# Measured durations in the list that orders the convolution block

## The chip, the cores and the metric

The kernel runs on one NeuronCore of a Trainium2 chip. The metric is the device time of one execution in microseconds (us); lower is better. The core has five engines that run side by side and meet through semaphores: TensorE (PE in the profile, its weight loads PEld), VectorE (DVE), ScalarE (ACT), GpSimd (POOL) and SyncE (SP). POOL and SP mostly issue DMAs here.

## The reference, cut to what matters

One step of a two-layer trunk over a prompt of 512 tokens and 8 x 4 decode tokens, model width 1024, all in float32. Layer 0 mixes tokens with a conformer convolution, layer 1 with stick-breaking attention; a gated feed-forward network with a small convolution follows each.

```python
def conformer_conv(h, past, w_in, b_in, w_dw, b_dw, ln_g, ln_b, w_out, b_out):
    u = h @ w_in + b_in
    a, gate = jnp.split(u, 2, axis=-1)
    glu = a * jax.nn.sigmoid(gate)
    ext = jnp.concatenate([past, glu], axis=1)
    y = causal_dwconv(ext, w_dw, b_dw)          # 31 taps, each channel by itself
    y = jax.nn.silu(layer_norm(y, ln_g, ln_b))
    return y @ w_out + b_out, ext[:, -(CONV_WIDTH - 1):]

# in run_trunk, for each layer
h = rms_norm(x, norm_mix[i]); x = x + mixer(h)
h = rms_norm(x, norm_ffn[i]); x = x + conv_ffn(h, ...)
```

The change touches only the order of layer 0's mixer, called the convolution block below.

## The kernel before, in words

Activations lie transposed: 128 channels on the partitions (a chunk; there are 8 chunks), tokens along the free dimension. The 544 tokens go in two halves, half 0 of 256 prompt tokens and half 1 of 256 prompt tokens and the 32 decode tokens. A weight tile of 1024 x 128 is a slot. Each is loaded in pairs as a 1 MB `raw` tile (two buffers), and split by ScalarE into a high part (L374) and by VectorE into a low part (L377); the low part of a pair's second slot triggers the next load (L337, from POOL in this block). A product of one slot and one half is 24 matmuls: high weights by high and low activations, low weights by high activations (L730 to L732). They are called projections here. Slots 0 to 15 are the input matrix, in groups of four for two chunks (two of values, two of gates); slots 16 to 23 are the output matrix.

What happens to a pair of projections, in order:

- the gate (`glu`): VectorE scales gate and value out of their PSUM banks (L763, L767), ScalarE takes the sigmoid (L765), VectorE multiplies (L769, for decode tokens L773) into `ext_p`;
- the 31 taps of the prompt tokens: chunks 0 and 1 on VectorE, one tap an instruction (L814, the last L818). Chunks 2 to 7 on TensorE: SP writes the chunk's half to DRAM (L832, a chunk write) and reads it back in four copies shifted against each other (L836, into one of four `rep` buffers; L839 clears a corner on VectorE), ScalarE builds diagonal weights (L853, 32 for a chunk, five buffers), and 32 matmuls on quarters of the array (L867) do the sum. Such a set is called a shift product here; there are 12, one for each chunk and half, and the profile counts two records for each of their matmuls. ScalarE evacuates it (L872). They share two PSUM banks, so each needs the evacuation of the one two places before it;
- the decode tokens' taps: a multiplication (L791) and a reduction (L796) on VectorE, a bias on ScalarE (L798);
- the sum over chunks for the layer norm (L884, `ysum`), the mean product on TensorE (L900), on VectorE the subtraction (L908), on ScalarE squares (L910), sums of pairs of them (L915), four variance products (L918), root (L922), reciprocal (L924), the multiplication (L929), silu (L931), the high and low parts (L933, L934), and the output projections of that half.

Nothing of this is ordered by hand. `Plan.op` records each piece with its engine, an assumed cost in us, and what it reads and writes. `Plan.run` then places all pieces in one greedy pass: each engine has its own time, a piece is ready when what it needs is done plus a hand-over time (`lag`: `LATENCY` of the engine that it comes from, and 0.12 more towards TensorE), and among ready pieces the earliest goes first, moved forward by the length of the chain behind it (`eager`, 0.12 for a dependent chain within VectorE). The pass issues the instructions in that order, and each engine's queue keeps it on the chip. `change` is an assumed price for a TensorE piece whose `form` (the way the array is divided) differs from that of the piece before; it also counts, times `CHANGE_BIAS` (3.0), against choosing such a piece. The convolution block's plan has not set it, so it is 0 there. One piece of a projection is six matmuls, one of a shift product 16. The feed-forward and attention blocks have plans of their own, with constants of their own.

Of the kernel before, what the change touches and what calls it, by code (L numbers as in the profile page):

```python
# [226 lines left out]
def tile_trunk(  # L227
# [8 lines left out]
    nc = tc.nc  # L236
    dve, act, pool, pe = nc.vector, nc.scalar, nc.gpsimd, nc.tensor
# [187 lines left out]
    def pcol(row, c):  # L425
        return prm[:, c, row:row + 1]
# [18 lines left out]
    def uid(s):  # L445
        _n[0] += 1
        return f"{s}_{_n[0]}"
# [152 lines left out]
    ext_p = conv.tile([P, NC, T], F32, name="ext_p")  # L600
# [84 lines left out]
    for i in range(2):  # L685
        ch0 = (PE_CHUNKS[0] + i * len(PE_CHUNKS) // 2) * P
        for m in range(8):
            nj = min(4, CW - 4 * m)
            pool.dma_start(out=trow[i][m * n_g:(m + 1) * n_g, :nj * 32].rearrange("g (j h) -> g j h", j=nj),
                          in_=conv_w_dw[0, 4 * m:4 * m + nj, ch0:ch0 + n_g * 32].rearrange("j (g h) -> g j h", h=32))  # L690
# [2 lines left out]


    plan = Plan(E_CONV, 0.12)
    STREAMS = (SA, SB)
    late = {}

    def buf(pool_, tag, shape, bufs):
        name = pool_ if isinstance(pool_, str) else None  # L700
        b = plan.tile(tag, bufs, lambda: late.get(name, pool_).tile(shape, F32, tag=tag, name=uid(tag), bufs=bufs))
        if name:
            b.after |= {late["op"]}
        return b
# [3 lines left out]
    def psum(tag):  # L708
        def make():
            if tag == "acc":  # L710
                taken.append(tag)
            return bank(tag, uid(tag))

        return plan.tile(tag, banks[tag], make)
# [4 lines left out]
    def product(slot, h):  # L719

        c0, n = STREAMS[h]
        pt = psum("acc")
        last = None
        for q in range(4):

            def f(q=q):
                hi, lo, _ = W.w[slot]
                o = pt()[:, :n]
                for k in (2 * q, 2 * q + 1):
                    pe.matmul(o, hi[:, k, :], XH[:, k, c0:c0 + n], start=(k == 0), stop=False)  # L730
                    pe.matmul(o, hi[:, k, :], XL[:, k, c0:c0 + n], start=False, stop=False)  # L731
                    pe.matmul(o, lo[:, k, :], XH[:, k, c0:c0 + n], start=False, stop=(k == NC - 1))  # L732

            last = plan.op("pe", 6 * (n / 2400 + 0.0025), f, w=[pt], follows=last,
                    r=[("slot", slot), ("slot", slot, q // 2)] + [(x, k, h) for x in ("XH", "XL") for k in (2 * q, 2 * q + 1)])
        if h:
            ahead = SPLIT_BUFS + (MORE if slot >= 2 * NC else 0)
            if slot + ahead < 2 * NC + NC + SPLIT_BUFS:
                prepare(slot + ahead, lambda low: W.free(low), [("slot", slot)])
        return pt  # L740

    def prepare(slot, begin, place):

        low = []
        raw = slot // 2
        plan.op("act", 0.95, lambda: begin(low), r=[("raw", slot)], w=[*place, ("slot", slot), "prep"])
        plan.op("dve", 1.135, lambda: low[0](), r=[("raw", slot)], w=[("slot", slot), "low"])
        if slot % 2:
            plan.op(f"raw{raw}", 5.4 if raw else 8.6, lambda: None, w=[("raw", slot + 2 * RAW_BUFS + i) for i in (-1, 0)], r=[("slot", slot)])
# [4 lines left out]
    def ext(c, *parts):  # L754

        return [("ext", c, i) for i in parts or range(4)]

    def glu(c, h, pa, pg):

        c0, n = STREAMS[h]  # L760
        r = rstd[:, c0:c0 + n]
# [63 lines left out]
    def shifted(c, h):  # L825


        lo = 256 * h
        w = RW + 2 + h
        d = plan.tile("glu", 4, lambda: scratch.tile([P, RW + 4], F32, tag="glu", name=uid("glu"), bufs=4))  # L830
        r = buf("taps", "rep", [P, 4, RW], REPB)
        plan.op("sp", 3.0, lambda: nc.sync.dma_start(out=d()[:, :w], in_=ext_p[:, c, lo:lo + w]),  # L832
                r=ext(c, 1, 2, 3) if h else ext(c, 0, 1), w=[d])
        for j in range(4):
            m = RW if j < 3 else RW - 1
            plan.op("sp", 3.5, lambda j=j, m=m: nc.sync.dma_start(  # L836
                out=r()[32 * j:32 * j + 32, :, :m], in_=d()[:, j:j + m].rearrange("(g h) t -> h g t", g=4)),
                r=[d, "taps"], w=[(r, j)])
        plan.op("dve", 0.07, lambda: dve.memset(r()[96:P, :, RW - 1:], 0.0), r=["taps"], w=[(r, 4)])  # L839
        return r  # L840
# [16 lines left out]
    def conv_tensor(c, h, r):  # L857
        lo = 256 * h
        wdg = diag[c]
        pt = psum("av")  # L860
        last = None
        for m0 in (0, 4):

            def f(m0=m0):
                for m in range(m0, m0 + 4):
                    for g in range(4):
                        pe.matmul(pt()[32 * g:32 * g + 32, 0:256], wdg()[:, g * 8 + m, :],  # L867
                                  r()[:, g, 4 * m:4 * m + 256], start=(m == 0), stop=(m == 7), skip_group_check=True)

            last = plan.op("pe", 2.05, f, follows=last, r=[(r, i) for i in range(5)] + ["taps", *((wdg, g) for g in range(0, 32, 4))],  # L870
                           w=[pt])
        plan.op("act", 0.36, lambda: act.activation(yc[:, c, lo:lo + 256], pt()[:, 0:256], AF.Identity,  # L872
                                                    bias=pcol(R_BDW, c)),
                r=[pt, "prm"], w=[("y", c, h)] + (ext(c, 1, 2) if h else ext(c, 0)))

    def add_sum(c, h):
        c0, n = STREAMS[h]
        if c == 0:
# [12 lines left out]
    def layer_norm(h):  # L891

        c0, n = STREAMS[h]
        cols = slice(c0, c0 + n)
# [68 lines left out]
    def incoming(h):  # L963
        c0, n = STREAMS[h]
        mine = blocks[2 * h:2 * h + 2 + h]
# [67 lines left out]
    def conv_in(c2, h):  # L1033
        s0 = 2 * c2
        pts = []
        for i in range(4):
            pts.append(product(s0 + i, h))
            if i > 1:
                glu(c2 + i - 2, h, pts[i - 2], pts[i])
# [38 lines left out]
    for c in range(0, NC, 2):  # L1078
        pt = psum("av")
# [8 lines left out]
        for cc in range(2):  # L1088
            plan.op("act", 0.33, lambda c=c, cc=cc, pt=pt: act.copy(
                ext_s[:, c + cc, :, 0:PAST], pt()[:, cc * 240:(cc + 1) * 240].rearrange("p (b t) -> p b t", b=NB)),  # L1090
                r=[pt, "junk"], w=[("past", c + cc)])
# [109 lines left out]
    def normed(c, h):  # L1201

        c0, n = STREAMS[h]
        sq = plan.tile("sq" if c else "sqa", 2, lambda: nrm.tile("sq" if c else "sqa", 2))
# [11 lines left out]
    for h, (c0, n) in enumerate(STREAMS):  # L1216
        if h:
            layer_norm(1)
        for g in (0, 4):
            for i in range(4):  # L1220
                c = g + i
                pt = product(s0 + c, h)
# [4 lines left out]
        if not h:  # L1227
# [6 lines left out]
    n = SA[1]  # L1234
    plan.op("pe", 0.53, lambda: pe.matmul(ms()[:, :n], mean_m, nrm.acc[0]()[:, :n], start=True, stop=True),
            r=[nrm.acc[0]], w=[ms])
    plan.op("act", 0.34, lambda: act.activation(rs()[:, :n], ms()[:, :n], AF.Sqrt, bias=eps_t[:, 0:1], scale=1.0),
            r=[ms, "table"], w=[rs])
    plan.op("dve", 1.7, lambda: dve.reciprocal(rs()[:, :n], rs()[:, :n]), w=[rs])
    for c in range(NC):  # L1240
# [3 lines left out]
                r=[rs, ("x", c, 0)], w=[u])  # L1244
# [4 lines left out]
            r=[u, ("XH", c, 0)], w=[("XL", c, 0)], lift=NLIFT)  # L1249
# [802 lines left out]
    plan = Plan()  # L2052
# [433 lines left out]
    for i, tag in enumerate(("acc", "z", "z", "one")):  # L2486
        pt = psum(tag)
        begun.append(pt)
        last = None
        for q in range(4):  # L2490
            last = plan.op("pe", 6 * SA[1] * COL, weighted(pt, o0 + i, 0, q), w=[pt], follows=last,
                           r=[("slot", o0 + i)] + [("X", k) for k in (2 * q, 2 * q + 1)])
# [3 lines left out]
    for j in range(2):  # L2496
        rows = slice(j * HD, (j + 1) * HD)
        hi, lo = (X[rows, :, SEQ:T].rearrange("p c (b i) -> p c b i", b=NB) for X in (XH, XL))
# [56 lines left out]
```

## Time and profile before

| | |
|---|---|
| time, median of 3 runs | 1274.54 us (1273.38 to 1275.0) |
| the profiled execution | 1274.43 us |
| its span, first to last instruction | 1272.7 us |
| granted TensorE clock, mean | 0.998 |
| convolution block in the span | up to about 219 us |
| TensorE busy in the span | 1259.1 us (99%) |
| VectorE, ScalarE busy in the span | 1002.8 us (79%), 717.7 us (56%) |

Times in the profile count from the span's first instruction. A row of the timeline has the start, the duration, the engine, the line of the kernel, the operation with the tiles it writes and reads, the shape and a count of merged instructions; in brackets stands how long the engine was idle before it and what ended that. Matmuls are pipelined, so the pace of TensorE is read from the distance of starts and not from durations. A row of the waits has who waited for whom, the total in us, how often, and the longest.

### The profile page before, as it was taken

The numbers are of one execution on the slowest core, as the hardware profiler recorded it, in microseconds if no ns is written. First come the engines' busy times: TensorE is split into PE (matmuls) and PEld (weight loads), VectorE is DVE, ScalarE is ACT, GpSimd is POOL, SyncE is SP. The second block draws the span as 40 slices with busy tenths as digits, with TensorE's granted clock in tenths as the row PEclk, the third lists the DMA queues.
The fourth block names the chain that finished last, engine by engine and source line by source line (L and its number), as shares of the span: only waits on it lengthen the run. The fifth ranks groups of instructions, "written<-read, shape, count | busy, mean of one in ns | idle before, by whom it ended". The sixth has DMA issues, their size and how long they took to land. (4 is left out here: it accounts for less than half of the span.)

```text
span 1272.7 us, 26479 instructions
## 1 busy us (share of the span) xinstructions
PE 1259.1 (99%) x10846; PEld 1209.1 (95%) x10846; DVE 1002.8 (79%) x1696; ACT 717.7 (56%) x1436; POOL 165.8 (13%) x291
## 2 busy tenths in 40 slices
PE   9999999999999999999999999999999999999998
PEld 8997789999999999999999888899999999999998
DVE  6999877888987886879865589766988987886863
ACT  6596574545655454445565488754645655454453
POOL 5000014111001000001042143200111001000000
PEclk9999999999999999999999999999999999999999
DMA  7464333023233232244354544342223233232221
GB/s 220 122 188 131 92 102 116 28 91 103 87 112 117 67 112 91 91 143 156 126 187 137 157 142 147 113 139 78 64 88 109 88 105 117 67 117 88 89 77 71
DMA packets 119180, 142.39 MB, mean 112 GB/s; under 512 B 5102, under 2 KB 110246, under 8 KB 118787
## 3 DMA queue, kind: packets, MB, share of 16 engines
q1 hardware_dynamic: 110350, 111.89, 28.3%
q0 software_dynamic: 8704, 28.80, 7.2%
q8 instruction: 85, 1.39, 0.5%
q14 instruction: 37, 0.30, 0.1%
q10 hardware_dynamic: 4, 0.01, 0.0%
HBM read 129.34 MB, written 12.18 MB: 111 GB/s over the span
## 5 line engine op out<-in xcount | busy, mean ns | idle before, releaser
L374 ACT CAST whi<-raw 128x1024 fp32r<-128x1024 f32 (+2 forms) x247 | 224.7, 913 | 118.0 <-PE av L1377 25.1
L377 DVE TENSOR_TENSOR wlo<-raw,whi 128x1024 fp32r<-128x1024 f32 (+2 forms) x247 | 258.5, 1049 | 28.6 <-ACT whi L374 27.2
L730 PE MATMUL acc<-XH,whi 128*128 128x288 f32 (+1 forms) x384 | 114.1, 297 | 0.0
L731 PE MATMUL acc<-XL,whi 128*128 128x288 f32 (+1 forms) x384 | 110.5, 288 | 0.1
L732 PE MATMUL acc<-XH,wlo 128*128 128x288 f32 (+1 forms) x384 | 110.3, 287 | 0.1
L1376 PE MATMUL av<-HH,whi 128*128 128x288 f32 (+1 forms) x280 | 83.2, 297 | 0.4 <-DVE xT L1691 0.4
L1602 PE MATMUL acc<-TH,wlo 128*128 128x272 f32 x288 | 83.0, 288 | 0.0
L1600 PE MATMUL acc<-TH,whi 128*128 128x272 f32 x288 | 82.8, 288 | 0.0
L1601 PE MATMUL acc<-TL,whi 128*128 128x272 f32 x288 | 82.7, 287 | 0.0
L1377 PE MATMUL av<-HL,whi 128*128 128x288 f32 (+1 forms) x280 | 82.6, 295 | 0.0
L2100 PE MATMUL acc<-XH,whi 128*128 128x256 f32 (+1 forms) x264 | 82.0, 311 | 0.6 <-ACT kT L2138 0.6
L1378 PE MATMUL av<-HH,wlo 128*128 128x288 f32 (+1 forms) x280 | 82.3, 294 | 0.0
L1636 ACT COPY G<-acc 128x272 f32<-128x272 f32 (+1 forms) x72 | 26.8, 372 | 94.7 <-PE acc L1602 94.7
L1376 PE MATMUL tr<-HH,whi 128*128 128x256 f32 (+1 forms) x280 | 79.1, 283 | 0.0
L1377 PE MATMUL tr<-HL,whi 128*128 128x256 f32 (+1 forms) x280 | 78.9, 282 | 0.0
L1378 PE MATMUL tr<-HH,wlo 128*128 128x256 f32 (+1 forms) x280 | 78.5, 280 | 0.0
L2102 PE MATMUL acc<-XH,wlo 128*128 128x256 f32 (+1 forms) x264 | 75.8, 287 | 0.0
L2101 PE MATMUL acc<-XL,whi 128*128 128x256 f32 (+1 forms) x264 | 75.8, 287 | 0.0
L730 PEld LDWEIGHTS acc<-XH,whi 128*128 128x128 f32 x384 | 72.2, 188 | 2.8 <-issue 1.6
L731 PEld LDWEIGHTS acc<-XL,whi 128*128 128x128 f32 x384 | 72.2, 188 | 1.0 <-DVE XL L982 0.3
L732 PEld LDWEIGHTS acc<-XH,wlo 128*128 128x128 f32 x384 | 72.1, 188 | 0.3 <-DVE wlo L377 0.3
L1539 DVE SCALAR_TENSOR_TENSOR cv<-G,fprm,cv 128x560 f32<-128x560 f32 x88 | 69.4, 796 | 0.5
(465 smaller groups left out, 4374.1 us busy)
## 6 DMA issues: line engine op xcount, KB each, us to landing
raw<-in_ffn_w_gate_dram SPq DMA_DIRECT2D x22, 1024.0 KB
raw<-in_ffn_w_up_dram SPq DMA_DIRECT2D x22, 1024.0 KB, 5.4
raw<-in_ffn_w_down_dram SPq DMA_DIRECT2D x24, 768.0 KB, 4.5
raw<-in_attn_w_qkv_dram SPq DMA_DIRECT2D x12, 1024.0 KB, 5.0
raw<-in_conv_w_in_dram POOLq DMA_DIRECT2D x6, 1024.0 KB, 6.5
rep<-glu SPq DMA_DIRECT2D x36, 142.0 KB, 3.6
raw<-in_conv_w_out_dram POOLq DMA_DIRECT2D x4, 1024.0 KB, 6.5
raw<-in_ffn_w_down_dram SPq DMA_DIRECT2D x8, 512.0 KB
```

The source lines that it names most:

```text
L374: act.copy(hi[:, k, :], src[:, k])
L377: dve.tensor_tensor(lo[:, k, :], src[:, k], hi[:, k, :], op=ALU.subtract)
L730: pe.matmul(o, hi[:, k, :], XH[:, k, c0:c0 + n], start=(k == 0), stop=False)
L731: pe.matmul(o, hi[:, k, :], XL[:, k, c0:c0 + n], start=False, stop=False)
L732: pe.matmul(o, lo[:, k, :], XH[:, k, c0:c0 + n], start=False, stop=(k == NC - 1))
L1376: pe.matmul(o, hi[:, j + k, :], xh, start=(start and k == 0), stop=False, **kw)
L1377: pe.matmul(o, hi[:, j + k, :], xl, start=False, stop=False, **kw)
L1378: pe.matmul(o, lo[:, j + k, :], xh, start=False, stop=(stop and k == len(xs) - 1), **kw)
L1600: pe.matmul(o, hi[:, j + k, :], xh, start=(start and k == 0), stop=False, **kw)
L1601: pe.matmul(o, hi[:, j + k, :], xl, start=False, stop=False, **kw)
L1602: pe.matmul(o, lo[:, j + k, :], xh, start=False, stop=(k == 3), **kw)
L2100: pe.matmul(o, hi[:, k, :], XH[:, k, c0:c0 + n], start=(k == 0), stop=False)
```

## The change

The plan of the convolution block gets hand-over times and a price for changes of form of its own, and three costs: a projection's six matmuls, a chunk write, and half a shift product, which is also marked with a form (`c32`).

```diff
     plan = Plan(E_CONV, 0.12)
+    plan.LATENCY = {"pe": 0.2, "dve": 0.22, "act": 0.2, "pool": 0.07, "sp": 0.1}
+    plan.change = 0.17
...
-            last = plan.op("pe", 6 * (n / 2400 + 0.0025), f, w=[pt], follows=last,
+            last = plan.op("pe", 6 * n * 0.46e-3, f, w=[pt], follows=last,
...
-        plan.op("sp", 3.0, lambda: nc.sync.dma_start(out=d()[:, :w], in_=ext_p[:, c, lo:lo + w]),
+        plan.op("sp", 5.0, lambda: nc.sync.dma_start(out=d()[:, :w], in_=ext_p[:, c, lo:lo + w]),
...
-            last = plan.op("pe", 2.05, f, follows=last, r=[(r, i) for i in range(5)] + ["taps", *((wdg, g) for g in range(0, 32, 4))],
-                           w=[pt])
+            last = plan.op("pe", 1.82, f, follows=last, r=[(r, i) for i in range(5)] + ["taps", *((wdg, g) for g in range(0, 32, 4))],
+                           w=[pt], form="c32")
```

Before, the hand-over from VectorE was 0.13 and from ScalarE 0.15. In numbers, six projection matmuls go from 0.655 to 0.707 (256 columns) and from 0.735 to 0.795 (288). No instruction is added or removed; the order on the engines moves. Up to line 695 the lines keep their numbers, behind that they are two higher in the changed kernel.

On TensorE, ahead of the mean product of the first half's layer norm (L900), the order before has five shift products in a row (chunk 3's half 1, and half 0 of chunks 4 to 7); three others stand alone further ahead, with 24 to 96 projection matmuls between them. The number behind a name is the buffer's.

```order
L867 MATMUL av_1746<-rep_1171,wdg_1080 32x256 x32
L867 MATMUL av_1811<-rep_1633,wdg_1100 32x256 x32
L867 MATMUL av_1861<-rep_1691,wdg_1239 32x256 x32
L867 MATMUL av_1910<-rep_1738,wdg_1518 32x256 x32
L867 MATMUL av_1960<-rep_1828,wdg_1708 32x256 x32
```

In the changed order this place has both halves of chunks 2 and 3, half 0 of chunks 4 to 7, half of chunk 4's half 1, and then the mean product (L902 there).

```order
L869 MATMUL av_1692<-rep_1097,wdg_996 32x256 x32
L869 MATMUL av_1741<-rep_1156,wdg_1180 32x256 x32
L869 MATMUL av_1790<-rep_1212,wdg_996 32x256 x32
L869 MATMUL av_1838<-rep_1273,wdg_1180 32x256 x32
L869 MATMUL av_1902<-rep_1759,wdg_1196 32x256 x32
L869 MATMUL av_1966<-rep_1808,wdg_1220 32x256 x32
L869 MATMUL av_2007<-rep_1855,wdg_1602 32x256 x32
L869 MATMUL av_2052<-rep_1919,wdg_1861 32x256 x32
L869 MATMUL av_2094<-rep_1983,wdg_1196 32x256 x16
L902 MATMUL tr_2114<-ysum,mean_m 128x256
```

66 projection matmuls that stood behind the run now stand ahead of it. Behind L902, with its four variance products (L920), 30 of them are left where 84 stood. The last three and a half shift products come in pieces of 16, 32 and 64 matmuls between and behind the variance products, where four came in one run of 128 behind all of them.

On ScalarE, the same place before: evacuations (L872) of chunk 2's half 1, chunk 3's half 1, and half 0 of chunks 4, 5 and 6, with the diagonals of chunk 7 (L853) and the decode tokens' bias (L798) between them.

```order
L872 ACTIVATE ext_p<-av_1645,prm 128x256
L853 ACTIVATE wdg_1708<-eye,tapc 128x32 x16
L765 ACTIVATE sg_1764<-sg_1764,prm 128x256
L853 ACTIVATE wdg_1708<-eye,tapc 128x32 x4
L798 ACTIVATE ext_p<-ext_p,prm 128x32
L853 ACTIVATE wdg_1708<-eye,tapc 128x32 x8
L872 ACTIVATE ext_p<-av_1746,prm 128x256
L853 ACTIVATE wdg_1708<-eye,tapc 128x32 x4
L798 ACTIVATE ext_p<-ext_p,prm 128x32
L872 ACTIVATE ext_p<-av_1811,prm 128x256
L798 ACTIVATE ext_p<-ext_p,prm 128x32
L872 ACTIVATE ext_p<-av_1861,prm 128x256
```

And now, from the evacuation of chunk 3's half 0 (L874) to that of chunk 5's half 0:

```order
L874 ACTIVATE ext_p<-av_1741,prm 128x256
L800 ACTIVATE ext_p<-ext_p,prm 128x32 x2
L874 ACTIVATE ext_p<-av_1790,prm 128x256
L855 ACTIVATE wdg_1861<-eye,tapc 128x32 x16
L874 ACTIVATE ext_p<-av_1838,prm 128x256
L855 ACTIVATE wdg_1861<-eye,tapc 128x32 x8
L800 ACTIVATE ext_p<-ext_p,prm 128x32
L855 ACTIVATE wdg_1861<-eye,tapc 128x32 x8
L874 ACTIVATE ext_p<-av_1902,prm 128x256
L874 ACTIVATE ext_p<-av_1966,prm 128x256
```

The evacuation of chunk 2's half 1 (`av_1790`) has two of the decode tokens' biases ahead of it, those of chunks 2 and 3, and the diagonals of chunk 7 stand between it and the evacuation of chunk 4's half 0 (`av_1902`).

On VectorE, from the reciprocal of the first half's layer norm to its low parts, before:

```order
L924 RECIPROCAL dwa_2215<-dwa_2215 128x256
L929 TENSOR_TENSOR ext_p<-ext_p,dwa_2215 128x256 x8
L839 MEMSET rep_2237 32x4
L796 TENSOR_REDUCE ext_p<-prod_2213 128x32
L884 TENSOR_TENSOR ysum<-ext_p,ysum 128x288
L377 TENSOR_TENSOR wlo_2188<-raw_1441,whi_2187 128x1024
L884 TENSOR_TENSOR ysum<-ext_p,ysum 128x288
L934 TENSOR_TENSOR XL<-ext_p,XH 128x256 x3
```

And now, to the first subtraction of the second half's layer norm (L910):

```order
L926 RECIPROCAL dwa_2281<-dwa_2281 128x256
L931 TENSOR_TENSOR ext_p<-ext_p,dwa_2281 128x256 x8
L886 TENSOR_TENSOR ysum<-ext_p,ysum 128x288
L936 TENSOR_TENSOR XL<-ext_p,XH 128x256 x2
L377 TENSOR_TENSOR wlo_2254<-raw_1896,whi_2253 128x1024
L936 TENSOR_TENSOR XL<-ext_p,XH 128x256 x4
L886 TENSOR_TENSOR ysum<-ext_p,ysum 128x288
L910 TENSOR_TENSOR ext_p<-ext_p,tr_2395 128x288 x6
```

A reduction, a weight split and a sum no longer stand between the multiplication (L931) and the first low parts (L936); one weight split stands behind the first two of those.

## The prediction

> **What bounds the kernel now.** I read the page's head first, then the busy time of each engine over five stretches of the convolution block, the only block whose order changes.
>
> ```profile
> span 1272.7 us, 26479 instructions
> ...
> 33.00:80.00 47.00, 47.00 (x384) 47.00 (x383) 42.96 (x86) 31.29 (x105) 3.54 (x4) 1.00 0.55 156
> 80.00:120.00 40.00, 40.00 (x480) 32.47 (x482) 38.22 (x74) 34.57 (x141) 1.76 (x2) 1.00 0.43 127
> 120.00:135.00 15.00, 13.84 (x236) 8.64 (x228) 14.05 (x21) 3.63 (x12) 0.00 (x0) 1.00 0.53 120
> 135.00:164.00 29.00, 27.73 (x350) 21.84 (x350) 23.40 (x46) 20.43 (x43) 1.77 (x2) 1.00 0.36 100
> 164.00:192.00 28.00, 27.53 (x217) 26.08 (x214) 20.62 (x43) 19.40 (x39) 4.44 (x6) 1.00 0.32 102
> ```
>
> After each stretch's length stand the busy times of PE, PEld, DVE, ACT and POOL, the granted clock and the DMA share. TensorE has no hole from 33 to 120 us and three small ones after it; the clock is full. A new order adds and removes no work, so it can only win what TensorE loses here: waits, and a price for each switch of array form. VectorE, 92 to 96% busy from 33 to 135 us, is close behind. Now TensorE's rows, which give pitches, switches and waits.
>
> ```profile
> 84.37 0.29 PE L730 MATMUL acc<-XH,whi 128*128 128x288 f32 x1
> 84.76 0.29 PE L730 MATMUL acc<-XH,whi 128*128 128x288 f32 x1
> ...
> 101.39 3.66 PE L867 MATMUL av<-rep,wdg 128*32 128x256 f32 x64
> 104.98 0.39 PE L730 MATMUL acc<-XH,whi 128*128 128x256 f32 x1
> ...
> 107.99 3.66 PE L867 MATMUL av<-rep,wdg 128*32 128x256 f32 x64
> ...
> 113.80 0.28 PE L730 MATMUL acc<-XH,whi 128*128 128x256 f32 x1
> 114.15 0.28 PE L730 MATMUL acc<-XH,whi 128*128 128x256 f32 x1
> 114.59 5.60 PE L867 MATMUL av<-rep,wdg 128*32 128x256 f32 x100
> ...
> 131.99 0.40 PE L730 MATMUL acc<-XH,whi 128*128 128x288 f32 x1
> ...
> 135.20 0.70 PE L900 MATMUL tr<-ysum,mean_m 128*128 128x256 f32 x2 [1.35 <-DVE ysum L884]
> ...
> 142.14 0.59 PE L918 MATMUL tr<-sqn,mean_m 128*128 128x256 f32 x2
> ...
> 144.16 0.59 PE L918 MATMUL tr<-sqn,mean_m 128*128 128x256 f32 x2
> ...
> 148.65 3.66 PE L867 MATMUL av<-rep,wdg 128*32 128x256 f32 x64
> ...
> 156.66 3.66 PE L867 MATMUL av<-rep,wdg 128*32 128x256 f32 x64 [0.90 <-DMA rep<-glu]
> ...
> 164.09 0.39 PE L730 MATMUL acc<-XH,whi 128*128 128x256 f32 x1
> 165.85 0.75 PE L900 MATMUL tr<-ysum,mean_m 128*128 128x288 f32 x2
> 170.31 0.75 PE L918 MATMUL tr<-sqn,mean_m 128*128 128x288 f32 x2 [0.21 <-DVE sqn L915]
> ```
>
> Every third projection matmul is an L730; two of them are 0.39 us apart at 288 columns and 0.35 at 256, so one projection matmul takes 0.13 us (0.132 over a long run) or 0.117 us. Five shift products from 114.59 to 131.99 take 17.40, 3.48 us each. One that stands alone takes 3.59 (101.39 to 104.98) and the 24 projections behind it 3.01 (104.98 to 107.99) where 24 x 0.117 is 2.81: a lone shift product costs **0.31 us** in switches.
>
> The waits: 12 projections at 131.99 reach L900 at 135.20, 3.21 where 1.59 would do, so **1.62** goes to the first layer norm. The four last shift products (from 148.65 to 164.09, 15.44) lose **1.5** against 4 x 3.48, most of it on a copy. 12 projections from 164.09 to 165.85 lose **0.36**, the 30 behind them **0.5** (4.46 to 170.31, less 3.51 and 0.4 for L900). That is 4.0 us.
>
> **Why the first wait is there.** VectorE and ScalarE run in order, and ScalarE frees the shift products' banks.
>
> ```profile
> DVE sg L763 <- PE acc L732: 2.0, 4, 0.6
> DVE va L767 <- PE acc L732: 0.6, 2, 0.3
> DVE wlo L377 <- ACT whi L374: 0.4, 1, 0.4
> DVE rstd L1013 <- PE tr L1010: 0.4, 1, 0.4
> ...
> 119.70 0.48 DVE L818 SCALAR_TENSOR_TENSOR ext_p<-ext_p,prm,dwh 128x256 f32<-128x256 f32 x1
> ...
> 130.20 1.19 DVE L796 TENSOR_REDUCE ext_p<-prod 128x32 f32<-128x992 f32 x1
> 131.30 1.18 DVE L791 TENSOR_TENSOR prod<-ext_s,prm 128x992 f32<-128x992 f32 x1
> ```
>
> ```profile
> 112.09 3.49 ACT L853 ACTIVATE wdg<-eye,tapc 128x32 f32<-128x32 f32 x16
> ...
> 131.47 0.32 ACT L798 ACTIVATE ext_p<-ext_p,prm 128x32 f32<-128x32 f32 x1 [2.87 <-DVE ext_p L796]
> 131.70 0.46 ACT L872 ACTIVATE ext_p<-av,prm 128x256 f32<-128x256 f32 x1
> ```
>
> The product of chunk 6 ended at 114.59 + 4 x 3.48 = 128.5, but its evacuation L872 ran at 131.70: ahead of it stood L798, which waited 2.87 us for VectorE's reduction L796. VectorE was late because it had waited 3.6 us from 33 to 120 (the first four rows and 0.2), mostly for projections.
>
> **The change, part by part.** *Switches.* Before, chunk 2's first half, chunk 3's first and chunk 2's second stand alone between projections; now nearly all projections come first, and eight and a half shift products follow in one run. Three lone ones go: 3 x 0.31 = **0.9 us won**. The three short pieces now between the first norm's variance products (L918) stand where projections stood, which paid for switching too (from the L918 at 142.14 to that at 144.16, 12 projections and one L918 of 0.24 take 2.02, not 1.83); I put them equal. [...]
>
> *First half's layer norm.* The shift products start at 114.59 - 3 x 3.59 (the lone ones) - 3 x 0.2 (the excess of what follows them) + 66 x 0.132 (projections that now come first) = 111.9; unhindered, four products later (3.48 each, 0.11 for the first) chunk 4 starts at 126.0, chunk 5 at 129.4, chunk 6 at 132.9. But L872 of chunk 2's second half now stands behind two L798, the second of which needs VectorE's reduction of chunk 3, and the bank it frees is chunk 4's. Against L818, which ended at 120.1, VectorE has 7.2 us more ahead of that reduction's end: 1.1 for one L796, 4 x 1.1 for chunks 2 and 3 (one L796 to the next instruction: 130.20 to 131.30), 1.3 for the gate of chunk 6, 0.4 for less interleaved taps. Its waits shrink: the order puts more tap steps ahead of each gate. The bounds are nothing saved and all 3.6; I take 1.9: of the 2.6 for projections the 1.2 of the latest (both L767 and one L763, of chunks 5 to 7, whose gates now come 2 to 8 us behind their projections) and half of the other 1.4. So 120.1 + 7.2 - 1.9 = 125.4; L798 and L872 end at 126.3. Behind them ScalarE has 16 diagonals (3.4 us by the row at 112.09), chunk 3's evacuation, 8 diagonals, an L798, 8 diagonals (1.7 each) and only then chunk 4's, done at 134.4, on whose bank chunk 6 waits: **1.5** beyond its 132.9, and this moves one for one with VectorE's lag (0 to 3.4). VectorE then has little left, so that the 8.8 us of shift products from there to L900 hide the last sum: 1.6 go, 1.5 come, **0.1 won**.
>
> *The late copies.* POOL and SP show what the 1.5 us were.
>
> ```profile
> 147.00 0.88 POOL L337 DMA_DIRECT2D raw<-in_conv_w_out_dram  x1 [50.27 <-DVE wlo L377]
> ...
> 149.83 0.34 SPq L832 DMA_DIRECT2D glu<-ext_p  x1
> 150.22 7.38 SPq L836 DMA_DIRECT2D rep<-glu  x6
> ...
> SPq L836 <- DMA glu<-ext_p: 6.0, 2, 4.6
> ```
>
> The 1 MB weight load at 147.00 runs while chunk 6 and 7 are written and copied; the longest wait for a chunk write is 4.6 us, the other 1.4. Now that load's trigger (the low part of slot 17) comes ahead of the norm, some 15 us sooner, and chunk 6's gate before the shift products. Chunk 7's stays late: ready at 149 (30 projections and two norm products behind L900, then its gate), its copies land at about 155 and are used at 157.9. **1.5 won**; with the slow write 3.2 us later, 0 to 0.5 is left.
>
> *The end of the first norm.* Its projections now follow VectorE closely.
>
> ```profile
> 153.21 1.74 DVE L924 RECIPROCAL dwa<-dwa 128x256 f32<-128x256 f32 x1
> 154.99 2.77 DVE L929 TENSOR_TENSOR ext_p<-ext_p,dwa 128x256 f32<-128x256 f32 x8
> ...
> 160.89 0.42 DVE L934 TENSOR_TENSOR XL<-ext_p,XH 128x256 fp32r<-128x256 f32 x1
> ```
>
> Before, 15 us of shift products covered this; now 7.1 stand behind the last L918. With L900 at 143.2, that L918 ends at 154.3, the shift products at 161.4 (164.09 before). L924 starts 0.9 behind the L918 (ScalarE's root), at 155.2, L929 at 156.9; with an L884 and two L934 the first two chunks are ready at 160.7, but a weight split (L377, 1.14) stands before chunks 2 and 3 (162.6, wanted 162.1), and the second L900 waits for ScalarE to evacuate chunk 7 (164.0, wanted 163.3). That is 1.2 where 0.36 was: **0.8 lost**. Behind the second L900 no weight split stands before L908 any more: of the 0.5 wait at 170.31, **0.2 won**. What waits behind the second norm hangs on chains that the order leaves as they are: **0**. The start (to 33 us) shifts a root and two diagonals ahead of the first weight split, 0.6 us, behind which the second split comes as before: 0, at most 0.6 lost; I take 0.
>
> Sum: 0.9 + 0.1 + 1.5 - 0.8 + 0.2 = 1.9 won. The profiled execution took 1274.43 us (span and 1.7 around it), the median is 1274.54, so **1272.5**. All that follows on TensorE starts sooner by as much.
>
> **Rivals.** *VectorE saves nothing* or chunk 7's write is slow again: chunk 6 waits 1.9 more, or up to 1.5 comes back, about **1274.4**. For it: the lag grew all through 33 to 120 us. Against: the gates lie further behind their projections. *Everything is covered*: VectorE saves all 3.6 (1.5 more), and the 1.2 at the first norm's end falls away: **1269.8**. *Slower by one place*: ScalarE's evacuation of chunk 2 behind L798. Each us of VectorE's lag is a us of TensorE there; 4.6 us beyond my 125.4 make it slower than the median by 0.2%, 2.55 us, which the measurement can just tell from no change: **1277.1**. [...] *The change does not do what it says* (the order moves, the bound does not): only the 0.9 of switches, **1273.5**.
>
> **How the numbers follow.** My forecast 0.45, nothing saved or slow write 0.18, switches alone 0.06, all covered 0.19, slower 0.12. Faster by over 0.2% means under 1272.0: all covered and some 0.16 of the forecast's part, 0.35. Slower 0.12, the rest 0.53. The range takes in the covered case, 1269.8, and on the other side the lag's bound, the start's 0.6 and a slow write together: 1272.5 + 1.9 + 0.6 + 1.5 = 1276.5.
>
> **What would show it.** Right: the first L900 at about 143, chunk 6 waiting 1.5 us on ScalarE, no wait on a copy, L900 again at 163 to 164.5, everything after it 2 us sooner. Wrong: a wait on L872 over 3 us, or on DMA in the last two products; the first norm's L900 before 142 would mean VectorE saved more.

## The result, and the profile after

| | before | after the change |
|---|---|---|
| median of 11 runs | 1273.62 us | **1270.88 us** |
| lowest, highest | 1273.13, 1275.0 | 1270.13, 1274.05 |
| span of the profiled execution | 1272.7 us | 1269.5 us |

The ratio is 0.9975, 95% interval 0.9967 to 0.9982: a quarter of a per cent faster. The forecast, 1272.5 us, was 1.6 us too high; the time lies inside the range. 0.9 of the 1.6 is the base, since the kernel before took 1273.62 us here and 1274.54 when the forecast was made. The gain itself was forecast at 1.9 us; it is 2.7 by these medians and 3.2 by the spans of the profiled executions. All of the 3.2 us between the two spans arise in the convolution block: the first matmul of the block behind it (L1376, now L1378) starts 3.2 us sooner, and nothing is won or lost after it.

The stretches of the convolution block after the change, with the same columns as before (length, busy times of PE, PEld, DVE, ACT, POOL, granted clock, DMA share, GB/s):

```profile
33.00:80.00 47.00, 47.00 (x384) 47.00 (x383) 45.07 (x92) 24.81 (x73) 3.54 (x4) 1.00 0.47 137
80.00:120.00 40.00, 40.00 (x395) 36.93 (x398) 39.15 (x70) 36.24 (x148) 1.77 (x2) 1.00 0.42 126
120.00:135.00 15.00, 15.00 (x284) 9.07 (x280) 12.50 (x21) 9.64 (x40) 0.88 (x1) 1.00 0.78 208
135.00:164.00 29.00, 28.21 (x413) 18.30 (x406) 22.36 (x46) 19.04 (x41) 0.88 (x1) 1.00 0.45 115
164.00:192.00 28.00, 28.00 (x224) 27.41 (x225) 22.11 (x44) 21.50 (x44) 4.43 (x6) 1.00 0.25 79
```

TensorE's hole from 120 to 135 us is gone (15.00 of 15.00, before 13.84), and so is that from 164 to 192. VectorE does more of its work ahead of 120 us (45.07 and 39.15, before 42.96 and 38.22) and has 2.5 us to spare from 120 to 135, where it had 1. That is the shape of the gain.

TensorE's rows after the change; L869, L902 and L920 are the shift products, the mean products and the variance products (L867, L900, L918 before):

```profile
112.64 3.66 PE L869 MATMUL av<-rep,wdg 128*32 128x256 f32 x64
...
142.13 0.70 PE L902 MATMUL tr<-ysum,mean_m 128*128 128x256 f32 x2
...
149.46 0.70 PE L920 MATMUL tr<-sqn,mean_m 128*128 128x256 f32 x2
150.08 3.66 PE L869 MATMUL av<-rep,wdg 128*32 128x256 f32 x64
153.68 0.70 PE L920 MATMUL tr<-sqn,mean_m 128*128 128x256 f32 x2
154.30 7.11 PE L869 MATMUL av<-rep,wdg 128*32 128x256 f32 x128
163.82 0.75 PE L902 MATMUL tr<-ysum,mean_m 128*128 128x288 f32 x2 [0.79 <-DVE ysum L886]
```

From 112.64 to 142.13 stand eight and a half shift products, 29.49 us or 8.5 x 3.47: **no wait at all**, neither chunk 6's 1.5 us nor the first mean product's. Why, the waits of VectorE from 33 to 120 us tell (us in all, times, longest):

```profile
DVE va L769 <- PE acc L734: 0.4, 1, 0.4
DVE dwh L816 <- ACT dwh L813: 0.2, 1, 0.2
```

0.6 us, where it was 3.6. So VectorE's reduction of chunk 3, and ScalarE's evacuations behind it, come early enough; here ScalarE's rows:

```profile
123.15 0.32 ACT L800 ACTIVATE ext_p<-ext_p,prm 128x32 f32<-128x32 f32 x1 [2.45 <-DVE ext_p L798]
123.37 0.46 ACT L874 ACTIVATE ext_p<-av,prm 128x256 f32<-128x256 f32 x1
...
131.87 0.45 ACT L874 ACTIVATE ext_p<-av,prm 128x256 f32<-128x256 f32 x1
133.64 0.47 ACT L874 ACTIVATE ext_p<-av,prm 128x256 f32<-128x256 f32 x1 [1.32 <-PE av L869]
```

ScalarE did wait for that reduction (2.45 us), as forecast, but until 123.1 and not 125.4. The evacuation on whose bank chunk 6 waits ended at 132.3, and chunk 6's product began at 133.6, when chunk 5's was done: 1.3 us to spare in place of 1.5 short.

### The profile page after: what moved, and what is told of

It is laid out like the page before. It is cut to its first block, busy times and chain, and to the rows that moved or that the text cites. A ratio compares the mean times of both kernels' runs of the same rounds, so it can differ in the third digit from the quotient of the medians.

```text
span 1269.5 us, 26475 instructions
## 1 busy us (share of the span) xinstructions
PE 1256.9 (99%) x10846; PEld 1207.8 (95%) x10846; DVE 1001.7 (79%) x1696; ACT 716.9 (56%) x1436; POOL 164.8 (13%) x291
## 5 line engine op out<-in xcount | busy, mean ns | idle before, releaser
L1378 PE MATMUL av<-HH,whi 128*128 128x288 f32 (+1 forms) x280 | 83.3, 297 | 0.4 <-DVE xT L1693 0.4
L1378 PE MATMUL tr<-HH,whi 128*128 128x256 f32 (+1 forms) x280 | 79.1, 283 | 0.0
```

The source lines that it names most:

```text
L1378: pe.matmul(o, hi[:, j + k, :], xh, start=(start and k == 0), stop=False, **kw)
```

## The experiments

Every kernel was timed in five rounds against the kernel before, and a ratio is to the kernel before in the same rounds. Two theories stood at the start: the gain comes from the **price of a change of form**, which gathers the shift products into one run, or from the **projections' true duration**, by which the planner puts the gates where the projections are really done.

### One number alone, or all but one

Price of a form alone:

```diff
+    plan.change = 0.17
...
-                           w=[pt])
+                           w=[pt], form="c32")
```

> Before plus the price of a change of form alone (0.17 us, shift products marked as a form of their own); all durations as before. TensorE's order in this version: eight and a half shift products in one run, as after the change, but 72 projections earlier; the first norm's variance products stand between projections, not between shift products. Theory A (the gathering into one run makes the gain: no lone shift products, chunk 6's gate ahead of the run, the weight load's trigger ahead of the norm): 2 to 3 us faster than before, ratio 0.9977 to 0.9985, and VectorE waits for projections less than 1.5 us from 33 to 120 us. Theory B (the measured projection cost makes it, because the planner then puts the gates where their projections are really done): nothing of it here, ratio 0.9995 to 1.0005, and VectorE still waits over 3 us.

Projections' duration alone:

```diff
-            last = plan.op("pe", 6 * (n / 2400 + 0.0025), f, w=[pt], follows=last,
+            last = plan.op("pe", 6 * n * 0.46e-3, f, w=[pt], follows=last,
```

> Before plus the projections' measured duration alone (0.46 ns a column and matmul in place of 0.417 and a constant). TensorE's order is nearly that of before: three lone shift products, five in a run, four behind the first norm. Theory A (the one run makes the gain): ratio 0.9995 to 1.0005, the three lone products still cost 0.9 us, the first norm's mean product still waits 1 us or more, the slow chunk write still comes. Theory B (the durations make it): VectorE's waits from 33 to 120 us fall from 3.6 us to under 1.5 us and the time by 1.5 us or more, ratio 0.9975 to 0.9988.

After the change, less the price of a form:

```diff
-    plan.change = 0.17
...
-                           w=[pt], form="c32")
+                           w=[pt])
```

> After the change without the price of a change of form; the five durations and the hand-overs as after. TensorE's order: two shift products together, two lone ones' worth apart, then four and a half in a run, four behind the first norm. Theory A (the one run makes the gain): 0 to 0.8 us faster than before, ratio 0.9994 to 1.0000, and the copies of the last chunk fall behind the weight load again. Theory B (the durations make it): 2 to 3 us faster, ratio 0.9976 to 0.9985.

After the change, less the projections' duration:

```diff
-            last = plan.op("pe", 6 * n * 0.46e-3, f, w=[pt], follows=last,
+            last = plan.op("pe", 6 * (n / 2400 + 0.0025), f, w=[pt], follows=last,
```

> After the change with the projections' duration as before. TensorE's order: 624 projections, then eight and a half shift products in one run, as after; the variance products between shift products and 24 projections ahead of the first of them. Theory A (the one run makes the gain): as after, 2 to 3.5 us faster than before, ratio 0.9972 to 0.9984. Theory B (the projections' duration makes it): VectorE waits 3 us or more from 33 to 120 us as before, chunk 6's shift product waits for ScalarE's evacuation of chunk 4 by 1.5 us or more, and at most 1.5 us are won, ratio 0.9988 to 1.0000.

After the change, less the chunk write's duration:

```diff
-        plan.op("sp", 5.0, lambda: nc.sync.dma_start(out=d()[:, :w], in_=ext_p[:, c, lo:lo + w]),
+        plan.op("sp", 3.0, lambda: nc.sync.dma_start(out=d()[:, :w], in_=ext_p[:, c, lo:lo + w]),
```

> After the change with the chunk write's duration as before (3.0). TensorE's order: eight and a half shift products in one run, but 66 projections (8.8 us) sooner than after; the first norm's variance products stand between projections. Theory A (a run pays only where it starts late enough for VectorE; sooner, chunk 6 waits for ScalarE behind VectorE, and the last chunk's copies run beside chunk 6's copies and a weight load): 2 us or more are lost in the run and 1 us or more in the last products, ratio to before 0.9990 to 1.0015. Theory B (one run without lone products and with no variance product among shift products, which cost 1.4 us after the change, is best wherever it starts): faster than after, ratio 0.9960 to 0.9970.

After the change, less the hand-overs:

```diff
-    plan.LATENCY = {"pe": 0.2, "dve": 0.22, "act": 0.2, "pool": 0.07, "sp": 0.1}
```

> After the change with the hand-overs between engines as before. TensorE's order up to the first norm is as after (624 projections, eight and a half shift products); the variance products stand between shorter pieces. Theory A (what counts is the run behind the projections and the gates at their true times, which the projections' duration and the price of a form give): as after within 1 us, ratio to before 0.9970 to 0.9984. Theory B (the hand-overs are needed as well): 1.5 us or more slower than after, ratio 0.9988 or more.

After the change, less the shift product's duration:

```diff
-            last = plan.op("pe", 1.82, f, follows=last, r=[...
+            last = plan.op("pe", 2.05, f, follows=last, r=[...
```

> After the change with the shift product's duration as before (2.05 a half). TensorE's order up to the first norm is as after; behind it the last shift products are in other pieces between the variance products. Theory A: as after within 0.7 us, ratio to before 0.9970 to 0.9981. Theory B (this duration carries part of the gain): 1.5 us or more slower than after.

| kernel | ratio to before, interval | VectorE's waits 33 to 120 us, of these for projections | where TensorE lost in the profiled execution (run and last products: over 3.48 each; elsewhere: over after) |
|---|---|---|---|
| form alone | 1.0017, 1.0008 to 1.0026 | 3.4, 2.9 | 2.4 in the run, 4.5 in the last products |
| projections alone | 1.0016, 1.0006 to 1.0025 | 2.8, 0 | 0.9 in three lone products, 4.5 in the last products (1.7 of it at half clock) |
| all but form | 0.9989, 0.9980 to 0.9998 | 0.6, 0.4 | 0.8 in lone products, 0.5 and 1.2 around the second mean product |
| all but projections | 1.0031, 1.0019 to 1.0043 | 4.9, 4.2 | 3.6 waited at the end of the second norm and at the next block's |
| all but chunk write | 1.0001, 0.9992 to 1.0010 | 0.7, 0.3 | 6.0 in the last products (1.4 of it at half clock) |
| all but hand-overs | 1.0010, 1.0001 to 1.0019 | 2.5, 0 | 0.8 in the run, 1.4 and 1.6 around the second mean product (the 1.6 at half clock) |
| all but shift product | 0.9979, 0.9970 to 0.9988 | 0.9, 0.7 | 0.7 at the second mean product |
| after | 0.9975, 0.9967 to 0.9982 | 0.6, 0.4 | |

Neither theory holds as it was put. Each of the two numbers that were tried alone makes the kernel slower. Leaving out one of four gives up about half of the gain (the price of a form) or all of it (projections, chunk write, and the hand-overs, whose theory B came true); leaving out the shift product's duration gives up little, its theory A. **The gain is not a sum of parts.** Some of what these kernels lost is lost to the clock, in the rows that say so; the last section returns to it. What holds is one piece of each theory. VectorE's waits go with the durations, not with the run. The kernel with the form's price alone:

```profile
DVE sg L764 <- PE acc L733: 2.6, 6, 0.6
...
DVE va L768 <- PE acc L733: 0.3, 1, 0.3
```

With the projections' duration alone, none of these are left, but waits for ScalarE and a row sum are:

```profile
DVE wlo L377 <- ACT whi L374: 1.6, 2, 1.1
DVE rstd L1013 <- PE tr L1010: 0.7, 1, 0.7
```

With both that duration and the hand-overs, 0.6 to 0.9 us is all (all but form, all but chunk write, all but shift product, after). Without the projections' duration, but with the rest, the most:

```profile
DVE va L769 <- PE acc L734: 2.2, 7, 0.5
DVE sg L765 <- PE acc L734: 2.0, 5, 0.6
```

In that kernel no evacuation stood behind a late reduction until 134.3 us, and the run of shift products lost nothing. Yet it is the slowest of these: TensorE waits at the end of the second half's layer norm (low parts, XL) and for the next block's norm (sums of squares, sqa):

```profile
190.87 0.70 PE L1237 MATMUL tr<-sqa,mean_m 128*128 128x256 f32 x2 [1.71 <-DVE sqa L1214]
...
198.08 0.40 PE L733 MATMUL acc<-XL,whi 128*128 128x288 f32 x1 [0.83 <-DVE XL L936]
...
199.85 0.40 PE L733 MATMUL acc<-XL,whi 128*128 128x288 f32 x1 [1.10 <-DVE XL L936]
```

That these waits come from VectorE's lag ahead of 120 us is not shown, and the rows speak against it: between 177.6 and 190.4 us VectorE stood idle for 6.0 us. The second norm's root came 3.2 us later than after the change (179.5 for 176.4), and ScalarE made the high parts of that half (L935) from 190.2 us on, behind squares of the next norm, where after the change it began at 186.2. The next block's mean product (L1237) stands ahead of all projections of that half, where twelve stand before it after the change. So what differs is the order around the second norm; how the projections' duration leads the plan there stays open.

The chunk write's duration does its work through the copies. Without it, the run starts 66 projections sooner, waits for nothing (29.49 us again: the 2 us expected there did not come), and chunk 6's second half is gated only behind it. SP's rows of that kernel, with chunk 6's write and copies and then chunk 7's:

```profile
145.00 0.34 SPq L834 DMA_DIRECT2D glu<-ext_p  x1
146.79 1.73 SPq L838 DMA_DIRECT2D rep<-glu  x4
149.81 0.34 SPq L834 DMA_DIRECT2D glu<-ext_p  x1
157.09 1.26 SPq L838 DMA_DIRECT2D rep<-glu  x3
```

and POOL's weight load and TensorE's last products:

```profile
146.56 0.88 POOL L337 DMA_DIRECT2D raw<-in_conv_w_out_dram  x1 [52.57 <-DVE wlo L377]
```

```profile
155.41 3.66 PE L869 MATMUL av<-rep,wdg 128*32 128x256 f32 x64 [1.44 <-DMA rep<-glu]
161.75 5.09 PE L869 MATMUL av<-rep,wdg 128*32 128x256 f32 x64 [2.68 <-DMA rep<-glu]
```

Chunk 7's write takes 7.3 us until its copies can be issued, beside a load of 1 MB and four copies, and the products wait 4.1 us; the last one is slow on top (5.09 for 3.66, see the last section).

### What makes the last chunk's copies late

The load alone was put back to where it collides, in the kernel after the change:

```diff
             if self.nraw >= len(raws):
                 return
+            if self.nraw == 10 and not self.go:
+                return
...
+                    if c == 1 and not h:
+                        pool.tensor_copy(late["dot"], acc()[:, 0:1])
+                        W.go = True
+                        W.load()
```

> After the change, with one weight load (1 MB, issued by POOL at 128.7 us) held back until the first norm's first sum is there, about 145 us, which is some 3.5 us ahead of the last chunk's write to memory, as in the kernels where that write was slow. A read of one column by POOL is added; the order of all other engines is as after. Theory A (the late copies are late because that load runs beside the write): the write takes about 6 us to its copies in place of 2.2, the copies land at about 159, and the last shift product, which starts at 157.8, waits 1.2 to 3 us: 1.0 to 3.0 us slower than after the change, ratio to before 0.9982 to 0.9998. Theory B (the write's slowness comes from the place in SP's queue, or is covered here): within 0.5 us of after, ratio 0.9971 to 0.9980.

Ratio 0.9977 (0.9968 to 0.9986): as after. POOL's row of the load, and SP's of the write and its copies:

```profile
145.85 0.89 POOL L340 DMA_DIRECT2D raw<-in_conv_w_out_dram  x1 [0.72 <-ACT sqn L915]
```

```profile
148.52 0.34 SPq L837 DMA_DIRECT2D glu<-ext_p  x1
152.44 1.73 SPq L841 DMA_DIRECT2D rep<-glu  x4
```

The write took 3.9 us until the copies were issued, where it is 2.2 after the change (148.34 to 150.53), not 6, and no product waited: this expectation missed. A load alone is not enough. In all four kernels where the write took 6 us or more (before 6.0, form alone 6.5, projections alone 6.3, all but chunk write 7.3), the load was issued 2.8 to 3.5 us ahead of it **and** the four copies of chunk 6 (142 KB each) from 3.3 us ahead to just behind; with the load 3.8 us ahead and two of the copies earlier still (all but form) it took 3.5. With the load ahead of it and no copies it took 3.9 us here; with chunk 6's copies ahead and the load 1.3 us behind it, 3.2 in the next experiment. So the long writes stand where both were issued close by; no run varied the bytes under way alone. Of the two reasons the prediction gave for its 1.5 us, the second, chunk 6's gate ahead of the shift products, is enough by itself. Two things that the views do not show stand in the traces' semaphores. Before the change, the 0.9 us wait at 156.66 was for chunk 6's own copies: issued from 147.2 to 150.7 us, the last landed at 156.5. And in form alone and projections alone, where the profile names a row of ScalarE, chunk 7's last copy landed 0.2 us ahead of the product that waited 2.5 and 2.6 us (at 162.2 and 160.5).

The other way round, the load was held back until the write is issued, in the kernel with the projections' duration alone:

```diff
+        def write():
+            nc.sync.dma_start(out=d()[:, :w], in_=ext_p[:, c, lo:lo + w])
+            if (c, h) == (7, 1):
+                pool.tensor_copy(late["dot"], ext_p[:, c, lo + 255:lo + 256])
+                W.go = True
+                W.load()
```

> Before plus the projections' duration alone, with the weight load that POOL issued at 145.9, 3.5 us ahead of the last chunk's write, held back until that write is issued at 149.4 (a read of one column by POOL is added). Theory A (the load beside the write makes the last product's 3.0 us wait): the copies come about 2 us after the write in place of 6.3, the wait goes, and the time falls by 2.4 to 3.2 us against that kernel's, ratio to before 0.9991 to 0.9997. Theory B: the copies stay late, or the load that is now later makes ScalarE wait for its weights by as much; the time stays, ratio 1.0008 to 1.0025.

Ratio 1.0028 (1.0018 to 1.0037), slower still than projections alone (1.0016). The write now took 3.2 us, but the load's reader stood on ScalarE ahead of an evacuation, which came only behind it, at 161.26:

```profile
158.72 1.04 ACT L377 CAST whi<-raw 128x1024 fp32r<-128x1024 f32 x1 [5.24 <-DMA raw<-in_conv_w_out_dram]
```

TensorE then waited 3.9 us for that evacuation. The second branch of theory B came true: a load that late is waited for itself.

### Is VectorE's lag paid one for one?

The sample products of chunk 3 are computed once more, or four times more, ahead of their reduction:

```diff
+        def total():
+            for _ in range(1 if c == 3 else 0):
+                mult()
+            dve.tensor_reduce(y, v(), axis=mybir.AxisListType.X, op=ALU.add)
```

> After the change, with chunk 3's sample products (128 x 992, 1.1 us on VectorE) computed once more ahead of their reduction, so VectorE is 1.1 us later there. Theory A (VectorE's lag moves one for one into chunk 6's wait once a slack of 1.1 us, from ScalarE's evacuation at 131.9 to the product's start at 133.6, is used up): 0 to 0.3 us slower than after, ratio to before 0.9973 to 0.9979. Theory B (VectorE's lag doesn't reach TensorE here): the same as after.

> The same with four more, 4.4 us on VectorE ahead of chunk 3's reduction. Theory A: chunk 6 waits 3.3 us for ScalarE's evacuation, the first mean product comes 3.3 us later, at about 145.4, and the time is 2.8 to 3.8 us over that of after, ratio to before 0.9997 to 1.0006. Theory B (the lag is absorbed, as in the kernel with all but the projections' duration, where VectorE waited 4.9 us and the run of shift products lost nothing): under 1 us over that of after, ratio 0.9973 to 0.9983.

With one: 0.9975 (0.9964 to 0.9985), as after, which both theories allow. With four: 1.0011 (1.0002 to 1.0020). TensorE's and ScalarE's rows with four (L874, L879, L805 are the shift products, their evacuation and the activation behind chunk 3's reduction):

```profile
128.27 7.41 PE L874 MATMUL av<-rep,wdg 128*32 128x256 f32 x128 [2.12 <-ACT ext_p L879]
136.76 8.84 PE L874 MATMUL av<-rep,wdg 128*32 128x256 f32 x160 [1.07 <-ACT ext_p L879]
145.53 0.70 PE L907 MATMUL tr<-ysum,mean_m 128*128 128x256 f32 x2
```

```profile
127.53 0.32 ACT L805 ACTIVATE ext_p<-ext_p,prm 128x32 f32<-128x32 f32 x1 [7.36 <-DVE ext_p L800]
```

The chain is the one forecast: reduction, activation, evacuation, bank. It stops two products, chunk 4's for 2.1 us and chunk 6's for 1.1, 3.2 in all (3.3 expected), and the first mean product comes at 145.5 (145.4 expected). From the run's start the mean product is 3.9 us later for 4.4 us of lag, and 0.9 later for 1.1: nearly one for one. In the execution with one more the run began 0.5 us sooner while VectorE did not, and that used up part of the slack. By the ratios the time with four is 4.6 us over after's, more than the 3.8 expected at most, while the profiled execution's span is 3.4 over. Its eleven times fall into two groups: five from 1274.1 to 1274.7, some 3 us over after's as expected, and six from 1275.9 to 1277.3. What may part them stands in the last section.

### A try at a better order

One part of the first norm's end was put by hand behind the evacuation that the second mean product waits for; `keep` holds a step back until the last sum has been issued:

```diff
+            if not h and c > 3:
+                high, low = keep(high), keep(low)
+                silu = keep(silu) if c > 5 else silu
```

> After the change, with a part of the first norm's end put by hand behind the evacuation of the last shift product: on ScalarE the high parts of chunks 4 and 5 and one activation, on VectorE the low parts of chunks 4 and 5 behind the last sum. All else is in the order of after. Theory A (the second mean product waits 1.0 us because that evacuation stands behind 1.1 us of the norm's work on ScalarE, 162.8 where the product ended at 161.4): the second mean product comes 0.8 us sooner, at about 163.0, and the time is 0.5 to 0.9 us under that of after, ratio to before 0.9967 to 0.9973. Theory B (the wait only moves to the projections that need the low parts, or to the second norm): within 0.3 us of after, ratio 0.9973 to 0.9978.

1270.58 us, ratio 0.9971 (0.9960 to 0.9983): the value lies in theory A's range, but the interval takes in both theories and after. The rows decide. TensorE's rows (L915 and L933 are the mean and variance products):

```profile
162.76 0.65 PE L915 MATMUL tr<-ysum,mean_m 128*128 128x288 f32 x2
...
167.38 0.75 PE L933 MATMUL tr<-sqn,mean_m 128*128 128x288 f32 x2 [0.48 <-DVE sqn L930]
```

The second mean product came 1.1 us sooner than after the change (1.0 counted from the first one), as theory A had it, but 0.5 us is waited at the next variance product already, and at the next block's norm 0.2 us is left, 0.1 of which was there at the first mean product. Theory B: ScalarE computes the second norm's squares behind two weight casts whose place did not change.

## Why the prediction was right, and where it was off

Between the two first mean products (135.20 before, 142.13 after) stand 54 more projections and half a shift product after the change, 54 x 0.132 + 1.74 = 8.9 us; 6.9 passed. Between the mean products of the two halves, the same work less takes 21.7 in place of 30.65 us. So:

| step of the prediction | forecast | measured |
|---|---|---|
| start, to 33 us | 0 | -0.7 |
| switches, three lone products | +0.9 | +0.9 (the run loses nothing) |
| first norm's wait: 1.6 go, 1.5 come | +0.1 | **+1.7** |
| late copies | +1.5 | +1.5 (no wait on a copy) |
| variance products between shift products | 0 | -0.7 |
| end of the first norm | -0.8 | -0.7 (second mean product at 163.8, forecast 164.0) |
| behind the second mean product | +0.2 | +1.2 |
| sum | 1.9 | 3.2 |

- **The step that was mis-sized** is "the bounds are nothing saved and all 3.6; I take 1.9". VectorE saved 3.0 and the reduction ended at 123.1 in place of 125.4. The mechanism behind it was right, as the added lag shows: 2.3 us less lag, and a run that began 0.7 us later than forecast, turned 1.5 us of wait into 1.3 us of slack. I had split the waits gate by gate from where each gate moved; the table of the kernels shows that they go or stay nearly as a whole, with the projections' duration for the waits for projections and with the hand-overs for the rest. The prediction called an L900 before 142 the sign that VectorE saved more; it came at 142.1, with 0.7 us lost at the start.
- **Late copies**: the size was right; of the two reasons one is enough. Most of the 1.5 us had been a wait for chunk 6's copies.
- **"I put them equal"**: a variance product between shift products takes 0.62 us from its start to the next row (149.46 to 150.08, 153.68 to 154.30), one between projections 0.24, which is 0.4 less, and the short pieces of shift products lose 0.1 each; against that stand the 0.2 that the projections behind each had paid before.
- **Behind the second mean product** I had counted 0.2 of the 0.5 us wait; all of it went, and 0.67 more at the first projections of the second half, which I had put at 0 because their chains are unchanged. They are not: twelve of these projections now stand ahead of the next block's first mean product (L1237, at 189.55), where six stood (L1235, at 191.85), and VectorE has all eight low parts of that half ahead of the next norm's reciprocal, where it had seven. Both are places in the order, and no run moved them alone.
- **The start** scatters. In six executions with the order of after (its own, the two with added lag, the late load, the two with other orders only behind the first norm) the run of shift products began between 112.1 and 112.8 us. Of the kernel before there is one trace, so whether the order costs anything there stays open.
- **The rivals.** The whole change does what "all covered" said of VectorE, and not what it said of the first norm's end: 12 projections take 2.48 us there (161.35 to 163.82), so 1.1 of the 1.2 us stayed. What made up for it was won behind the second mean product, where the forecast had only 0.2. The slower one, ScalarE's evacuation behind chunk 3's reduction, is real: four more products bring it about, at its place.
- **A reading**: VectorE was 91 to 96% busy from 33 to 135 us, not 92 to 96.

## What to carry to other kernels

A list scheduler's durations act together: here one true number alone, or four of the five, could be no better than none or worse, so such a table is best corrected as a whole and measured as a whole. To see what an order is worth, add up first how long the second-busiest engine waits; here its lag moved nearly one for one (3.9 us for 4.4) into the bound engine once a buffer hung on it, and where the slack ends is a number in the trace. The order decides whether one does: in all but projections VectorE waited 4.9 us and the run lost nothing. A transfer's duration belongs to its place: the same chunk write took 1.8 to 7.3 us here until its copies were issued, 6 us or more in the four kernels that issued a 1 MB load 2.8 to 3.5 us ahead of it and the four copies of another chunk around it.

## What the runs showed of the hardware

**TensorE's clock was halved behind four holes of 2.15 to 3.86 us.** After the wait of 2.15 us in the kernel without the hand-overs (columns as in the stretches above; the clock stands third from the end):

```profile
162.50:166.20 3.70, 1.78 (x16) 1.48 (x12) 1.94 (x6) 3.70 (x10) 0.00 (x0) 1.00 0.00 0
166.20:167.70 1.50, 1.27 (x8) 1.17 (x9) 1.02 (x2) 1.50 (x4) 0.00 (x0) 1.00 0.00 0
167.70:171.20 3.50, 3.50 (x19) 3.50 (x18) 3.36 (x10) 3.48 (x6) 0.00 (x0) 0.51 0.48 142
```

TensorE was back at work at 166.4, and 1.3 us later it ran for 3.4 us at half the clock: 30 projections took 5.28 us where after the change they took 3.71. The same came behind holes of 2.62 us (projections alone), 2.68 us (all but chunk write, the product of 5.09 above) and 3.86 us (load behind the write), for 3.4 us each, at a price of 1.4 to 1.7 us. It did not come behind 2.53 us (form alone), 2.12 us (four more products) and 1.71 us (all but projections, at 189 us); the stretch of the first:

```profile
162.40:168.00 5.60, 5.60 (x79) 4.26 (x80) 3.67 (x8) 4.06 (x7) 0.00 (x0) 1.00 0.56 187
```

So the hole's length alone does not tell: half the clock followed 2.15 us and did not follow 2.53. Counted from the hole's start, it began after 2.2 us (all but chunk write), 3.0 us (projections alone) and 3.5 us (without the hand-overs, load behind the write). At the end of the program, behind 1.6 us of matmuls of a single column (L1959, L1961 after the change), it began 1.0 us after the last matmul in the kernel before and 3.3 us after it in the changed one. What sets the moment is not shown.

Kernels with such holes scatter by 2.4 to 5.9 us between executions (form alone 3.7, projections alone 5.9, four more products 3.2, in two groups some 1.8 us apart), a held norm's end by 0.8 and all but shift product by 1.1. The mean granted clock on record of each execution fits a dip that comes in some executions and not in others: projections alone has 0.998 or 0.999 in its three fastest (1274.1 to 1274.5 us) and 0.996 in its two slowest (1277.1 and 1280.1); with four more products the five shorter executions have 0.997 to 0.999 and the six longer ones 0.996 to 0.998; after the change ten have 0.998 or 0.999 and the one at 1274.05 us has 0.995. Since each kernel has one trace, where the dips of the other executions lie is not shown. It also means that a part of what those kernels lost against the kernel before is the price of a dip, and not of the order alone.
